# A hybrid streaming-encoder layer on one core: the low parts of the sixteen meta tokens move into the rows of high x

## The chip, the cores and the metric

The kernel runs on one core of one Trainium2 chip. The metric is the device time of one execution in microseconds, the median over several runs. The core has a matrix engine (PE, which loads weights and streams columns of a moving operand past them into PSUM), a vector engine (DVE), a scalar engine (ACT), a general engine (POOL), an engine that only issues transfers (SP), and sixteen DMA engines.

## The reference, cut to what matters

One layer, 512 real tokens behind 16 learned meta tokens, model width 2048. Everything the change touches is the first projection:

```python
meta = jnp.broadcast_to(meta_tokens[None], (bsz, N_META, D_MODEL))
h_res = jnp.concatenate([meta, x], axis=1)          # 16 + 512 rows
hn = _rmsnorm(h_res, norm_in_g[l])
P = hn @ w_in[l]                                    # 2048 -> 65 * 128 columns
Pr, Pc = P[..., :RW_COLS], P[..., RW_COLS:]         # group A: r, k, v, g, two low-rank inputs; group B: B, C, h, gc
...
prev = jnp.pad(Pr[:, :-1], ((0, 0), (1, 0), (0, 0)))
Pr = Pr + (prev - Pr) * mu_shift[l]                 # token shift: token t needs t - 1
...                                                 # RWKV-7 recurrence over r, k, v; gated width-3 convolution over B, C, h, gc
h_res = h_res + mix @ w_out[l]
out = _rmsnorm(h_res, norm_f_g)[:, N_META:]
```

The meta tokens are dropped from the output, so not every projection needs all of them. k, v and the low-rank inputs feed the recurrent state and need all 16. r, g, C and h need only the last two (token shift and convolution look one and two tokens back). B and gc need none.

## The kernel before, in words

**The projection.** Its 65 output tiles of 128 columns are computed one after the other in an order written out as a table (`plan`). Weights are the stationary operand (128 x 128), x is the moving one. Both are fp32 numbers cut into a high and a low part, because a product of two such parts is accurate enough only when three of the four cross products are added: high w by high x, high w by low x, low w by high x. So each of the 16 slices of the contraction (`kt`) takes three matmuls for each column range (`steps`, L319 to L331). The high and low parts of x stand in SBUF for the whole kernel: `xh` and `xl`, 16 rows of 640 numbers per partition each, in each row the 512 real columns first, then the last two meta tokens, then the first fourteen.

**The ranges.** A tile goes to PSUM in one or two banks. k, v and the low-rank tile use `FULL`: columns 0 to 256, and 256 to 528 (256 real and 16 meta). r, g, C and h use `TAIL`: 0 to 256, and 256 to 514. B and gc use `REAL`: 0 to 512 in one bank. There are 17 tiles of the first kind, 32 of the second and 16 of the third. For one tile four slices of the first range are done, then four of the second, four times over; so matmuls of one width stand in chains of twelve.

**Leaving PSUM.** `scaled` (L346) multiplies a tile by the row of token scales `rs` on DVE, real columns and the two groups of meta columns apart, since these go to the front of the result. ACT and DVE then do the token shift, the convolution or the gates.

**The first 50 us.** Four tiles (`lora`, k0, r0, B0) are computed side by side, slice by slice, while x and the first weights arrive. SP issues the transfers in the order of the text: one array `front` in four pieces (the first slice of x with gains and a first weight, three more weights, the second slice with four weights, slices 2 and 3 with eight), then weights and the other slices. ACT and DVE cut x (`split_x`, L205) and weights (`split_piece`, L225) in an order written by hand; ACT also squares x and DVE adds the squares into `accd` for the token scales (`square_x`, L213).

**Order of the rest.** PE runs one hand-made stream: small matmuls of the attention-like parts (`prepare`, `invert`, `recur`) are put into the stream of the projection, and `fill(ns)` issues that many nanoseconds of projection matmuls (counted as 0.43 ns per column) between two steps of them, so that ACT and DVE have time to bring what the next step needs. DVE, ACT and POOL queues outside the hand-ordered stretches are set by a scheduler. From about 841 us on the output projection follows, in the Winograd-like form of seven products; the change does not touch it.

Of the kernel before, what the change touches and what calls it, by code (L numbers as in the profile page):

```python
# [18 lines left out]
P = 128  # L19
# [58 lines left out]
def hymba_kernel(ctx: ExitStack, tc: tile.TileContext, xt, xtok, front, w_in, w_out, pv, lup, cst, msk, gf, out):  # L78
# [75 lines left out]
    xl = xp.tile([P, KT, XROW], F32R, name="xl")  # L154
# [44 lines left out]
    def load_x(tag, a, n):  # L199
        t = view(tag, n * L)  # L200
        nc.sync.dma_start(t.rearrange("p (k l) -> p k l", k=n), xt[:, a : a + n, :])
        for k in range(n):
            raw[a + k] = t[:, k * L : (k + 1) * L]

    def split_x(kt, cols=slice(0, L)):  # L205
        gain = ng[:, kt : kt + 1]
        nc.scalar.activation(xh[:, kt, cols], raw[kt][:, cols], AF.Copy, scale=gain)
        return nc.vector.scalar_tensor_tensor(
            out=xl[:, kt, cols], in0=raw[kt][:, cols], scalar=gain, in1=xh[:, kt, cols].bitcast(F32),
            op0=ALU.mult, op1=ALU.subtract,  # L210
        ).ins

    def square_x(kt, first=False):  # L213
        sq = accd if first else tr(f"sqx{kt}")[:, 0:L]
        nc.scalar.activation(sq, raw[kt], AF.Square)
        if not first:
            nc.vector.tensor_tensor(out=accd, in0=accd, in1=sq, op=ALU.add)
# [15 lines left out]
    F0, F1, F2 = KT + P + L, 4 * P + L, 8 * P + 2 * L  # L233
    fr = [view("bt", F0), view("r0", 3 * P), view("bk", F1), view("gt0", F2)]
# [5 lines left out]
    raw[0], raw[1] = fr[0][:, KT + P : F0], fr[2][:, 4 * P : F1]  # L240
    for k in range(2):
        raw[2 + k] = fr[3][:, 8 * P + k * L : 8 * P + (k + 1) * L]
# [8 lines left out]
    with tc.manual_schedule(engines={mybir.EngineType.DVE, mybir.EngineType.Activation}):  # L251
        split_piece(0, 0, fr[0][:, KT : KT + P])
        split_x(0, slice(0, L // 2))
        split_x(0, slice(L // 2, L))
        for n in (1, 2, 3):
            split_piece(n, 0, fr[1][:, (n - 1) * P : n * P])
        split_x(1)
# [16 lines left out]
        square_x(1)  # L274
        head = split_x(8)
# [38 lines left out]
    FULL = ((0, HALF), (HALF, L))  # L314
    TAIL = ((0, HALF), (HALF, SEQ + 2))
    REAL = ((0, SEQ),)
    PLACED = ((0, SEQ, META), (SEQ, SEQ + 2, META - 2), (SEQ + 2, L, 0))

    def steps(ps, ranges, k4, q, ks=range(4), rs_=range(2)):  # L319
        hi, lo = quarters[q]  # L320
        for r, (a, b) in enumerate(ranges):
            if r not in rs_:
                continue
            for k in ks:
                kt = 4 * k4 + k
                w = slice(k * P, (k + 1) * P)
                for n, (ww, xx) in enumerate(((hi, xh), (hi, xl), (lo, xh))):
                    nc.tensor.matmul(  # L328
                        ps[r], ww[:, w], xx[:, kt, a:b], start=(kt == 0 and n == 0), stop=(kt == KT - 1 and n == 2)
# [16 lines left out]
    def scaled(ranges, ps, dst, base):  # L346
        for (a, b), p in zip(ranges, ps):
            for c, d, t in PLACED:
                c0, d0 = max(a, c), min(b, d)
                if c0 < d0:  # L350
                    o = t + c0 - c - base
                    nc.vector.tensor_tensor(
                        out=dst[:, o : o + d0 - c0], in0=p[:, c0 - a : d0 - a], in1=rs[:, c0:d0], op=ALU.mult
                    )
# [128 lines left out]
    def mains():  # L483
# [5 lines left out]
        for k in range(4):  # L489
            for n, (ps, rg) in enumerate(four):  # L490
                if k == n == 0:
                    hi, lo = quarters[0]
                    for ww, xx, first in ((hi, xh, True), (lo, xh, False), (hi, xl, False)):
                        for p, (a, b) in zip(ps, rg):
                            nc.tensor.matmul(p, ww[:, 0:P], xx[:, 0, a:b], start=first, stop=False)
# [131 lines left out]
    def prepare(i):  # L627
# [7 lines left out]
        fill(FW["start"] if i else 6700)  # L635
# [40 lines left out]
        shift = {0: 2000, 1: 2500, 3: -4000}.get(i, 0)  # L676
# [31 lines left out]
        fill(FW["gram2"] - shift)  # L708
# [757 lines left out]
def _layout(i):  # L1466
# [4 lines left out]
    xt = hres.reshape(L, KT, P).transpose(2, 1, 0)  # L1471
    w = np.asarray(i["w_in"])[0].reshape(KT, P, 65, P).transpose(2, 1, 0, 3).reshape(65, P, DM)
# [28 lines left out]
    front = [pv[:, V_NG : V_NG + KT], first[0][:, 0], xt[:, 0]] + [t[:, 0] for t in first[1:]]  # L1501
# [25 lines left out]
```

## Time and profile before

| | |
|---|---|
| median of 3 runs | 1002.05 us (1001.93 to 1002.06) |
| profiled execution, its own time | 1003.54 us |
| its span, first to last instruction | 1001.7 us, 1.84 us less than its time |
| granted TensorE clock over the span | 0.998 |
| matmuls / weight loads in it | 9723 / 9723 |
| ACT, POOL busy | 393.5 us (39%), 272.3 us (27%) |
| HBM | 137.44 MB read, 36.35 MB written, 173 GB/s over the span |

How to read it: weight loads (PEld) overlap the matmuls, so the two busy times of the matrix engine are not added. The duration that the profile gives one matmul runs from its issue to its modelled end, some 280 ns for 256 columns, while the next one starts after less than half of that; so what a matmul costs is read from the distance between starts, in the timeline, and not from its duration. In the timeline consecutive instructions of one line and the same tiles are merged into one row with a count (x2).

### The profile page before, as it was taken

The page shows a single profiled execution, that of the slowest core. Times are in us where ns is not written, and L with a number is a line of the kernel's source. Part 1 is how long each engine was busy: PE and PEld are TensorE (multiplying, and loading weights), DVE is VectorE, ACT ScalarE, POOL GpSimd, SP SyncE. Part 2 cuts the span into 40 slices and gives each one's busy share as a digit, 9 for nine tenths or more (in the row PEclk, how much of TensorE's full clock was granted, in tenths as well). Part 3 has the DMA queues.
Part 4 walks back from the last instruction along what each step waited for, and adds up shares of the span by engine and source line. Part 5 has one row for each costly group of instructions (what it writes and reads, how often), then busy time and mean ns, then how long its engine had stood idle before and what let it go on. Part 6 is the DMA issues. An engine that isn't in the chain of part 4 may idle for free.

```text
span 1001.7 us, 23771 instructions
## 1 busy us (share of the span) xinstructions
PE 989.9 (99%) x9723; PEld 913.8 (91%) x9723; DVE 687.3 (69%) x1313; ACT 393.5 (39%) x729; POOL 272.3 (27%) x286
## 2 busy tenths in 40 slices
PE   9999999999999999999999999999999999999996
PEld 8999999999998999998999998979888898888886
DVE  7687975588765579744669744335454597999995
ACT  7553423344323434322434322223222325646553
POOL 0123423225332424233423222223332333001001
PEclk9999999999999999999999999999999999999999
DMA  9526576455664373854274846978673698788644
GB/s 335 153 73 167 128 200 162 109 145 126 164 171 149 101 184 105 206 147 119 85 193 102 202 140 175 342 228 255 198 233 86 173 280 228 215 283 228 144 103 168
DMA packets 185181, 175.35 MB, mean 175 GB/s; under 512 B 121584, under 2 KB 142832, under 8 KB 184560
## 3 DMA queue, kind: packets, MB, share of 16 engines
q1 hardware_dynamic: 182480, 164.92, 57.1%
q0 software_dynamic: 2304, 8.39, 4.9%
q8 instruction: 76, 1.25, 0.5%
q10 hardware_dynamic: 288, 0.52, 0.1%
q14 instruction: 33, 0.27, 0.1%
HBM read 137.44 MB, written 36.35 MB: 173 GB/s over the span
## 4 chain that ended last, share of the span: by engine, by line
PE 68%; DVE 1%; DMA 1%; issue 0%; SPq 0%; ACT 0%; DVEq 0%; POOL 0%
PE ps_gc L328 8%; PE M L1243 8%; PE ps_B L328 7%; PE ps_h L328 7%; PE ps_C L328 6%; PE ps_k L328 5%; PE ps_v L328 5%; PE ps_g L328 5%; PE ps_r L328 5%; PE P L1243 4%; PE Q L1243 2%; PE zy L1010 1%; PE zs L1006 1%; PE rz L954 1%; PE g L682 1%; PE end L1450 1%
## 5 line engine op out<-in xcount | busy, mean ns | idle before, releaser
L135 POOL TENSOR_TENSOR w<-wr,w 128x512 fp32r<-128x512 f32 x119 | 174.3, 1466 | 349.7 <-ACT w L134 290.5
L134 ACT CAST w<-wr 128x512 fp32r<-128x512 f32 x252 | 152.8, 618 | 281.9 <-PE ps_k L328 45.4
L135 DVE TENSOR_TENSOR w<-wr,w 128x512 fp32r<-128x512 f32 x133 | 98.7, 747 | 105.5 <-ACT w L134 105.2
L328 PE MATMUL ps_k<-xh,w 128*128 128x256 f32 (+1 forms) x512 | 95.5, 285 | 0.0
L328 PE MATMUL ps_r<-xh,w 128*128 128x256 f32 (+1 forms) x512 | 95.2, 282 | 0.0
L328 PE MATMUL ps_v<-xh,w 128*128 128x272 f32 (+1 forms) x512 | 95.2, 284 | 0.0
L328 PE MATMUL ps_h<-xh,w 128*128 128x258 f32 (+1 forms) x512 | 94.0, 283 | 0.0
L328 PE MATMUL ps_C<-xh,w 128*128 128x258 f32 (+1 forms) x512 | 93.2, 282 | 0.0
L328 PE MATMUL ps_g<-xh,w 128*128 128x258 f32 (+1 forms) x512 | 91.9, 281 | 0.2 <-DVE gt L692 0.2
L328 PE MATMUL ps_B<-xh,w 128*128 128x512 f32 x256 | 83.5, 395 | 0.1
L328 PE MATMUL ps_gc<-xh,w 128*128 128x512 f32 x256 | 81.5, 393 | 0.0
L328 PEld LDWEIGHTS ps_r<-xh,w 128*128 128x128 f32 x512 | 80.4, 190 | 0.3
L328 PEld LDWEIGHTS ps_k<-xh,w 128*128 128x128 f32 x512 | 80.2, 189 | 0.5
L328 PEld LDWEIGHTS ps_h<-xh,w 128*128 128x128 f32 x512 | 79.7, 189 | 0.7
L328 PEld LDWEIGHTS ps_v<-xh,w 128*128 128x128 f32 x512 | 80.1, 189 | 0.3
L328 PEld LDWEIGHTS ps_C<-xh,w 128*128 128x128 f32 x512 | 79.7, 189 | 0.6
L328 PEld LDWEIGHTS ps_g<-xh,w 128*128 128x128 f32 x512 | 79.3, 190 | 0.6 <-issue 0.4
L328 PE MATMUL ps_k<-xl,w 128*128 128x256 f32 (+1 forms) x256 | 72.9, 285 | 0.0
L328 PE MATMUL ps_v<-xl,w 128*128 128x256 f32 (+1 forms) x256 | 72.6, 284 | 0.0
L328 PE MATMUL ps_g<-xl,w 128*128 128x256 f32 (+1 forms) x256 | 72.5, 283 | 0.0
L328 PE MATMUL ps_r<-xl,w 128*128 128x256 f32 (+1 forms) x256 | 72.3, 283 | 0.0
L328 PE MATMUL ps_C<-xl,w 128*128 128x256 f32 (+1 forms) x256 | 72.0, 281 | 0.0
(320 smaller groups left out, 2264.6 us busy)
## 6 DMA issues: line engine op xcount, KB each, us to landing
wr<-in_w_in_dram SPq DMA_DIRECT2D x126, 512.0 KB
ct<-opd SPq DMA_DIRECT2D x64, 288.0 KB
wo<-in_w_out_dram SPq DMA_DIRECT2D x21, 512.0 KB
x<-in_w_out_dram POOLq DMA_DIRECT2D x16, 512.0 KB, 5.7
opd<-ar SPq DMA_DIRECT2D x8, 576.0 KB
opd<-gt SPq DMA_DIRECT2D x16, 288.0 KB
opd<-bt SPq DMA_DIRECT2D x64, 64.0 KB
x<-in_w_out_dram SPq DMA_DIRECT2D x8, 512.0 KB
```

Source lines behind the costliest of these rows:

```text
L134: nc.scalar.copy(hi, rq)
L135: low[q] = eng.tensor_tensor(out=lo, in0=rq, in1=hi.bitcast(F32), op=ALU.subtract).ins
L328: nc.tensor.matmul(ps[r], ww[:, w], xx[:, kt, a:b], start=(kt == 0 and n == 0), stop=(kt == KT - 1 and n == 2))
L682: nc.tensor.matmul(z[h][:, c - c0], bk[hs, c, h : h + 2, :].rearrange("p a s -> p (a s)"), ar[hs, c].rearrange("p a s -> p (a s)"), start= ...
L954: nc.tensor.matmul(z[e][ho if e else hs, 0, k], t[hs, o : o + CH], t[hs, O_V : O_V + CH] if part else st[hs, 4 * e + k], start=(part == 0 ...
L1006: nc.tensor.matmul(d[hs, j], w, x[hs], start=(a == 0), stop=(a == b - 1))
L1010: nc.tensor.matmul(d[ho, j], t[hs, o : o + CH], x[hs], start=(a == 0), stop=(a == b - 1))
L1243: nc.tensor.matmul(bank[s], left(prod, jj, m, s), w, start=(jj == 0 and n == 0), stop=(jj == 7 and n == 2))
L1450: nc.tensor.matmul(ends[part], left("M2", jj, m, 1), w[:, cols], start=(jj == 0 and n == 0), stop=(jj == 7 and n == 2))
```

## The change

The row of `xh` becomes: 512 real columns, the high parts of the last two meta tokens, their low parts, the high parts of the first fourteen, their low parts (544 numbers in the same 640). `xl` keeps only the real columns, 512 to a row. The new function `passes` gives the three matmuls of a slice for a range: high w by `xh` over high and low meta columns (260 or 288 wide), high w by `xl` over the 256 real columns, low w by `xh` up to the last high meta column (258 or 274; the latter also covers the two low columns in between). In the last slice the widest comes last. So the high-by-low product of a meta token lies in PSUM columns of its own, and `scaled` adds the pair with a TENSOR_REDUCE on DVE before it multiplies with `rs`.

At the start, the meta columns of all slices arrive in one piece (`metax`, issued third); `split_meta` multiplies them with the gains and cuts them for slices 1 to 15 in one DVE multiplication and two ACT/DVE pairs. Slice 0 brings its own. Real columns are then cut and squared 512 wide, the squares of the meta columns are summed by a reduce (`square_meta`). Three `fill` amounts of the first head pair move 1 us of projection work from behind the decay scan to ahead of the low-rank product.

```diff
-    xl = xp.tile([P, KT, XROW], F32R, name="xl")
+    xl = xp.tile([P, KT, SEQ], F32R, name="xl")
...
+    HI_A, LO_A, HI_B, LO_B = (slice(*c) for c in ((SEQ, SEQ + 2), (SEQ + 2, SEQ + 4), (SEQ + 4, L + 2), (L + 2, L + META)))
...
+    def split_meta(ks):
+        g = metag[:, ks]
+        nc.vector.tensor_tensor(
+            out=g, in0=metax[:, ks], in1=ng[:, ks].unsqueeze(2).to_broadcast([P, g.shape[1], META]), op=ALU.mult
+        )
+        for t, h, l in ((slice(0, 2), HI_A, LO_A), (slice(2, META), HI_B, LO_B)):
+            nc.scalar.copy(xh[:, ks, h], g[:, :, t])
+            nc.vector.tensor_tensor(out=xh[:, ks, l], in0=g[:, :, t], in1=xh[:, ks, h].bitcast(F32), op=ALU.subtract)
...
+    def square_meta():
+        sq = tr("sqm")[:, 0 : KT * META].rearrange("p (k t) -> p k t", t=META)
+        nc.scalar.activation(sq, metax, AF.Square)
+        nc.vector.tensor_reduce(out=accd[:, SEQ:L], in_=sq.rearrange("p k t -> p t k"), op=ALU.add, axis=AX.X)
...
-    fr = [view("bt", F0), view("r0", 3 * P), view("bk", F1), view("gt0", F2)]
+    fr = [view("bt", F0), view("r0", 3 * P), metax.rearrange("p k t -> p (k t)"), view("bk", F1), view("gt0", F2)]
...
         split_piece(0, 0, fr[0][:, KT : KT + P])
-        split_x(0, slice(0, L // 2))
-        split_x(0, slice(L // 2, L))
+        split_x(0, slice(0, SEQ // 2))
+        x0 = fr[0][:, KT + P : F0]
+        for h, c in ((slice(SEQ // 2, SEQ + 2), slice(SEQ // 2, SEQ + 2)), (HI_B, slice(SEQ + 2, L))):
+            nc.scalar.activation(xh[:, 0, h], x0[:, c], AF.Copy, scale=ng[:, 0:1])
+        real = slice(SEQ // 2, SEQ)
+        for d, c, h in ((xl[:, 0, real], real, real), (xh[:, 0, LO_A], HI_A, HI_A), (xh[:, 0, LO_B], slice(SEQ + 2, L), HI_B)):
+            nc.vector.scalar_tensor_tensor(
+                out=d, in0=x0[:, c], scalar=ng[:, 0:1], in1=xh[:, 0, h].bitcast(F32), op0=ALU.mult, op1=ALU.subtract
+            )
         for n in (1, 2, 3):
             split_piece(n, 0, fr[1][:, (n - 1) * P : n * P])
+        split_meta(slice(1, KT))
         split_x(1)
...
-    FULL = ((0, HALF), (HALF, L))
-    TAIL = ((0, HALF), (HALF, SEQ + 2))
+    FULL = ((0, HALF), (HALF, L + META))
+    TAIL = ((0, HALF), (HALF, SEQ + 4))
     REAL = ((0, SEQ),)
-    PLACED = ((0, SEQ, META), (SEQ, SEQ + 2, META - 2), (SEQ + 2, L, 0))
+
+    def passes(q, r, last=False):
+        (hi, lo), (a, b) = quarters[q], r
+        mid = min(b, SEQ)
+        end = {SEQ + 4: SEQ + 2, L + META: L + 2}.get(b, b)
+        p = [(hi, xh, a, b), (hi, xl, a, mid), (lo, xh, a, end)]
+        return p[1:] + p[:1] if last else p
...
-                for n, (ww, xx) in enumerate(((hi, xh), (hi, xl), (lo, xh))):
+                for n, (ww, xx, a, b) in enumerate(passes(q, part, kt == KT - 1)):
                     nc.tensor.matmul(
-                        ps[r], ww[:, w], xx[:, kt, a:b], start=(kt == 0 and n == 0), stop=(kt == KT - 1 and n == 2)
+                        ps[r][:, 0 : b - a], ww[:, w], xx[:, kt, a:b], start=(kt == 0 and n == 0),
+                        stop=(kt == KT - 1 and n == 2),
                     )
...
         for (a, b), p in zip(ranges, ps):
-            for c, d, t in PLACED:
-                c0, d0 = max(a, c), min(b, d)
-                if c0 < d0:
-                    o = t + c0 - c - base
+            m, o = min(b, SEQ), META + a - base
+            nc.vector.tensor_tensor(out=dst[:, o : o + m - a], in0=p[:, 0 : m - a], in1=rs[:, a:m], op=ALU.mult)
+            for t, n, h, c in ((META - 2, 2, SEQ, SEQ), (0, META - 2, SEQ + 4, SEQ + 2)):
+                if b >= h + 2 * n:
+                    e = tp.tile([P, META], F32, tag="tl", name="tl", bufs=4)[:, 0:n]
+                    nc.vector.tensor_reduce(
+                        out=e, in_=p[:, h - a : h - a + 2 * n].rearrange("p (a t) -> p t a", a=2), op=ALU.add, axis=AX.X
+                    )
                     nc.vector.tensor_tensor(
-                        out=dst[:, o : o + d0 - c0], in0=p[:, c0 - a : d0 - a], in1=rs[:, c0:d0], op=ALU.mult
+                        out=dst[:, t - base : t - base + n], in0=e, in1=rs[:, c : c + n], op=ALU.mult
                     )
...
-        fill(FW["start"] if i else 6700)
+        fill(FW["start"] if i else 7700)
...
-        shift = {0: 2000, 1: 2500, 3: -4000}.get(i, 0)
+        shift = {0: 1000, 1: 2500, 3: -4000}.get(i, 0)
...
-        fill(FW["gram2"] - shift)
+        fill(FW["gram2"] - shift - 1000 * (i == 0))
```

**What moves on PE.** The second range of tile C0, before: `ps_C_1` is its second bank, `w` the slot that holds the high and low part of the weights.

```order
L328 MATMUL ps_C_1_5669<-xh,w_5336 128x258
L328 MATMUL ps_C_1_5669<-xl,w_5336 128x258
L328 MATMUL ps_C_1_5669<-xh,w_5336 128x258 x2
L328 MATMUL ps_C_1_5669<-xl,w_5336 128x258
L328 MATMUL ps_C_1_5669<-xh,w_5336 128x258 x2
```

The same place now; in the k, v and low-rank tiles 288, 256 and 274 stand for 260, 256 and 258.

```order
L361 MATMUL ps_C_1_5767<-xh,w_5430 128x260
L361 MATMUL ps_C_1_5767<-xl,w_5430 128x256
L361 MATMUL ps_C_1_5767<-xh,w_5430 128x258
L361 MATMUL ps_C_1_5767<-xh,w_5430 128x260
L361 MATMUL ps_C_1_5767<-xl,w_5430 128x256
```

The number of matmuls is the same; a chain of twelve equal widths has become a cycle of three widths.

**What moves on DVE at the start**, before: from the first cut of x to the second slice's (`xl<-in_bk`). `in_bt`, `in_r` and `in_bk` are the buffers in which the pieces of `front` arrive.

```order
L208 SCALAR_TENSOR_TENSOR xl<-in_bt,xh 128x264 x2
L228 TENSOR_TENSOR w_144<-in_r_148,w_144 128x128
L228 TENSOR_TENSOR w_145<-in_r_148,w_145 128x128
L228 TENSOR_TENSOR w_146<-in_r_148,w_146 128x128
L208 SCALAR_TENSOR_TENSOR xl<-in_bk,in_bt,xh 128x528
```

The same stretch now:

```order
L210 SCALAR_TENSOR_TENSOR xl<-in_bt,xh 128x256
L278 SCALAR_TENSOR_TENSOR xl<-in_bt,xh 128x256
L278 SCALAR_TENSOR_TENSOR xh<-in_bt,xh 128x2
L278 SCALAR_TENSOR_TENSOR xh<-in_bt,xh 128x14
L244 TENSOR_TENSOR w_144<-in_r_150,w_144 128x128
L244 TENSOR_TENSOR w_145<-in_r_150,w_145 128x128
L244 TENSOR_TENSOR w_146<-in_r_150,w_146 128x128
L217 TENSOR_TENSOR metag<-metax,in_bt 128x240
L222 TENSOR_TENSOR xh<-metag,xh 128x15x2
L222 TENSOR_TENSOR xh<-metag,xh 128x15x14
L210 SCALAR_TENSOR_TENSOR xl<-in_bk,in_bt,xh 128x512
```

Two short cuts of slice 0 and the three instructions of `split_meta` now stand ahead of the second slice; on ACT the two copies of `split_meta` stand between the same neighbours.

35 lines of the change are left out of this document (20 added, 15 removed).

## The prediction

> **What bounds the kernel now.** I read the page first, then the engine waits, then the chain that ended last, then the timeline of PE.
>
> ```profile
> span 1001.7 us, 23771 instructions
> PE 989.9 (99%) x9723; PEld 913.8 (91%) x9723; DVE 687.3 (69%) x1313; ACT 393.5 (39%) x729; POOL 272.3 (27%) x286
> PE pwarm L187 <- DVE cold L184: 1.4, 1, 1.4
> PE zy L1010 <- issue: 1.3, 1, 1.3
> 53.50:618.00 564.50, 564.13 (x5419) 541.48 (x5418) 384.88 (x820) 207.26 (x384) 179.15 (x186) 1.00 0.56 145
> ```
>
> The second PE row is its longest wait after the start, and in the 564.5 us of the middle (columns: PE, PEld, DVE, ACT, POOL) PE shows no gap while DVE is busy 384.88 us. So PE's own stream of matmuls sets the end, and the change is worth what it does to the distance between starts. Four whole tiles from the chain that ended last:
>
> ```profile
> 468.15 11.58 PE ps_k L328 x96
> 530.94 11.53 PE ps_v L328 x96
> 568.47 11.25 PE ps_C L328 x96
> 786.21 10.88 PE ps_gc L328 x48
> ```
>
> gc: 10.88 / 48 = 226.7 ns for 512 columns. C streams 0.4% more columns than gc and takes 3.4% longer. The timeline (first column the start in us) tells which width is dear:
>
> ```profile
> 358.34 0.29 PE L328 MATMUL ps_k<-xl,w 128*128 128x272 f32 x1
> ...
> 359.45 0.29 PE L328 MATMUL ps_k<-xl,w 128*128 128x272 f32 x1
> ...
> 361.16 0.28 PE L328 MATMUL ps_k<-xl,w 128*128 128x256 f32 x1
> ...
> 361.87 0.28 PE L328 MATMUL ps_k<-xl,w 128*128 128x256 f32 x1
> ...
> 419.39 0.28 PE L328 MATMUL ps_C<-xl,w 128*128 128x256 f32 x1
> ...
> 420.41 0.28 PE L328 MATMUL ps_C<-xl,w 128*128 128x256 f32 x1
> ...
> 420.75 0.28 PE L328 MATMUL ps_C<-xl,w 128*128 128x258 f32 x1
> ...
> 421.84 0.29 PE L328 MATMUL ps_C<-xl,w 128*128 128x258 f32 x1
> ```
>
> The matmul with low x is every third one, so from row to row nine starts lie between (six in the second pair). In C: 1.02 / 9 = 113.3 ns for 256 columns, 1.09 / 9 = 121.1 ns for 258. Two columns more cost 7.8 ns. In k: 1.11 / 9 = 123.3 ns for 272, and 0.71 / 6 = 118.3 ns for 256. So 256 columns have a short distance (113) and a long one (118), and both hold for whole chains. 48 x 113.3 + 48 x 121.1 = 11.25 us and 48 x (118.3 + 123.3) = 11.60 us: the tiles are explained. From 272 to 512 a column costs (226.7 - 123.3) / 240 = 0.43 ns; what the change can win is the step just above 256, not columns.
>
> **The change part by part.** The number of matmuls and weight loads stays. TAIL streams 260 + 256 + 258 = 774 columns a slice, as 3 x 258 before; FULL 288 + 256 + 274 = 818 against 816. There are 32 TAIL tiles with 16 slices (512 steps) and 17 FULL ones (272 steps).
>
> *TAIL.* Before 3 x 121.1 = 363.3 ns. Now 258 stays at 121.1, 260 is 121.1 + 2 x 0.43 = 122.0. The open term is a lone 256 between wider ones; the nearest rows are two of the low-rank product (`tz`, 256 wide) between 272s of v:
>
> ```profile
> 62.22 0.28 PE L571 MATMUL tz<-la,luh 128*128 128x256 f32 x1
> 62.34 0.28 PE L572 MATMUL tz<-la,lul 128*128 128x256 f32 x1
> 62.46 0.28 PE L328 MATMUL ps_v<-xl,w 128*128 128x272 f32 x1
> 62.58 0.41 PE L328 MATMUL ps_v<-xh,w 128*128 128x272 f32 x2
> ```
>
> 0.36 us for two 256s and one 272 leaves (360 - 123.3) / 2 = 118.4 each. Bounds 113.3 and 118.4; I take 116, since the neighbours here are nearer to 256 than there. 122.0 + 116 + 121.1 = 359.1: -4.2 ns a step, **-2.15 us** for 512 (bounds -0.9 and -3.5).
>
> *FULL.* Before 369.9 ns. 274 is 123.3 + 0.9 = 124.2. For 288, the line from 272 gives 123.3 + 16 x 0.43 = 130.2; the only 288s of the trace stand on two-column weights:
>
> ```profile
> 359.81 0.30 PE L714 MATMUL n_misc<-sq_h,ones 128*2 128x288 f32 x1
> ...
> 360.34 0.40 PE L717 MATMUL zb<-rk_h,ones 128*128 128x512 f32 x1
> ```
>
> Four in 0.53 us are 132.5 ns. I take 131.3: 131.3 + 116 + 124.2 = 371.5, +1.6 a step, **+0.44 us** for 272 (bounds: 130.2 + 113.3 + 124.2 gives -0.6, 132.5 + 118.4 + 124.2 gives +1.4). The 16 columns of low meta that are moved beside the high ones are streamed all the same; only their place changes.
>
> *The first range.* Its 256-wide chains are not edited, but a chain's distance depends on what ran before it. After twelve 272s it is 118.3 (k above). After a mere pair of 272s (the low-rank product in v at 59.7 us) it is
>
> ```profile
> 59.72 0.29 PE L572 MATMUL tz<-la,lul 128*128 128x272 f32 x1
> ...
> 60.08 0.28 PE L328 MATMUL ps_v<-xl,w 128*128 128x256 f32 x1
> ...
> 60.76 0.28 PE L328 MATMUL ps_v<-xl,w 128*128 128x256 f32 x1
> ```
>
> 0.68 / 6 = 113.3. After the change no chain of twelve wide ones is left; each cycle holds a 256. For FULL (17 x 48 = 816 matmuls) the bounds are no change and -5 ns each, less about a fifth that are short already (v's tile is shorter than k's): -3.2 us. For TAIL (32 x 48 = 1536) it is no change or up to +5 ns each, +7.7 us, if the mixed cycle locks the chain behind it in the long distance. I take **-0.7 us**: the pair of 272s is nearest to the new cycle and speaks for short, but k's whole tile at 118 says that the long distance keeps itself up.
>
> *The first 12 us.* ACT, DVE, PE, then the DMA view of the first 14 us (forty slices of 0.35 us, and the mean):
>
> ```profile
> 9.66 0.74 ACT L207 ACTIVATE xh<-in_gt,in_bt 128x528 fp32r<-128x528 f32 x1 [2.50 <-DMA in_gt<-in_front_dram]
> 6.40 0.77 DVE L208 SCALAR_TENSOR_TENSOR xl<-in_bk,in_bt,xh 128x528 fp32r<-128x528 f32 x1 [0.23 <-ACT xh L207]
> 8.09 0.28 PE L328 MATMUL ps_lora<-xl,w 128*128 128x256 f32 x1
> 10.84 0.28 PE L328 MATMUL ps_lora<-xh,w 128*128 128x256 f32 x1
> 11.25 0.39 PE L328 MATMUL ps_lora<-xl,w 128*128 128x256 f32 x1
> 11.59 0.51 PE L328 MATMUL ps_lora<-xh,w 128*128 128x256 f32 x2
> GB/s 0 0 0 0 8 108 154 361 379 402 418 405 428 416 273 238 261 333 404 357 452 332 284 183 200 223 273 402 331 392 459 459 416 378 394 340 416 398 416 372
> DMA packets 1250, 4.22 MB, mean 302 GB/s; under 512 B 132, under 2 KB 260, under 8 KB 994
> ```
>
> Slice 2 is what PE waits for: 0.41 + 0.34 us between starts instead of 2 x 0.12, so 0.5 us lost, because its transfer lands at 9.66. Now 256 columns of meta (131 KB) go ahead of it, and 48 columns (25 KB) are saved: 106 KB at the 302 GB/s of the first 14 us is 0.35 us. Slice 1 is late too: two short cuts (0.15 us each), then the DVE product of 240 columns (0.42 us), two ACT copies (0.3 and 0.4), a DVE subtraction (0.4) ahead of the cut of slice 1, which then ends near 9.0 in place of 7.17, while PE asks for it at 8.09. That stall of 0.7 to 0.9 us takes the place of the one at slice 2, not of nothing. Together **+0.45 us** (bounds: the transfer alone, at the 400 GB/s that most slices from 3 us on reach, +0.27; both in full, +0.9).
>
> *Leaving PSUM.* 66 reduces more (two for each FULL tile, one for each TAIL tile) on DVE, in the class of
>
> ```profile
> L789 DVE TENSOR_REDUCE y<-prod 72x4 f32<-72x8 f32 x32 | 5.0, 156 | 0.9
> L352 DVE TENSOR_TENSOR pr_k<-ps_k,rs 128x14 f32<-128x14 f32 x8 | 1.3, 161 | 0.0
> ```
>
> 66 x 0.16 = 10.5 us of DVE, hidden under PE: DVE is idle a third of the middle, and two pairs of banks let PE run a tile (11 us) ahead. Queued behind a tile's multiplication are the shift and the products of the next head pair, later by 0.3 us. The place with least cover is the first pair, where the low-rank product waits for lora's shift; the 1 us of `fill` that is moved ahead of it is cover for that. **+0.1 us**; without cover 0.3 us for each of eight pairs, +2.4. Squares and cuts of x are 16 columns narrower and the reduce of `square_meta` takes that back: 0. The shorter rows of `xl` (512 in place of 640) cost nothing in any row: 0.
>
> Sum: -2.15 + 0.44 - 0.7 + 0.45 + 0.1 = -1.86 us on the span of 1001.7, so 999.8. The profiled execution has 1.84 us around its span; the median of the runs, 1002.05, lies 1.5 us under that execution, and I carry the difference over to it: **1000.2 us**.
>
> **The rivals.** *The short distance everywhere* (996 to 998): lone 256s at 113.3 and FULL's first chains short, -3.5 - 0.6 - 3.2 + 0.3 = -7.0 in full, about -5 for most of it: 997. For it: the pair in v, after which the chain is short. Against: the `tz` rows at 118.
>
> *The long distance everywhere* (slower): a 256 behind the mixed cycle stays at 118.3 through its chain of twelve, in TAIL tiles too, where it is 113.3 now. With a share s of TAIL's chains locked the time moves by -1.2 + 7.7 s: it decides from s = 0.15 on, is measurable from 0.41, and gives 1004.7 at one half, 1008.6 at all. For it: k, where it never leaves that state. Against: chains behind 258s, the closest width, are short in every C tile.
>
> *Columns alone count* (the change does not do what it says): what 258 pays over 256 is a price of the change of width or of the phase, so a cycle of three widths pays it again on each. Then 2 x 0.43 x 272 = +0.2, with +0.45 and +0.1: 1002.8. For it: the `tz` rows, where 256 gained only 5 of 10 ns. The Trainium skill has this as a rule (TensorE: Matmul & The Clock Gate, "Wait — 56ns, not 53.3ns?"): the distance is the columns at 2.4 GHz plus about 2.5 ns, whatever the width. By it 256, 258 and 512 would take 109.2, 110.0 and 215.8 ns; the trace has 113.3, 121.1 and 226.7, so it agrees for none of them, and the measured step decides against it here.
>
> **How the numbers follow.** Forecast 0.36, short everywhere 0.24, long everywhere 0.26, columns alone 0.14. About 0.2%, 2 us, is what a measurement can tell from no change. The forecast's own range is 998.8 to 1001.6, with 0.14 of its 0.36 below 1000.05; short everywhere is all faster; long everywhere is 0.21 slower and 0.05 within; columns alone 0.12 within and 0.02 slower. Faster 0.38, within 0.39, slower 0.23. The range 996 to 1005 leaves out the extreme third of each outer rival.
>
> **What would show it.** In the chain, a tile of C at 48 x 113.3 + 16 x 359.1 = 11.18 us against 11.25, k at 48 x 117.5 + 16 x 371.5 = 11.58. In the timeline: the row of `xl` at 256 with 116 ns to the next start, and whether the chains of twelve run at 113 or 118. At the start: PE's stall at slice 1 and not at slice 2, slice 3 some 0.45 us later. The forecast is wrong if C tiles take 11.4 us or more, or if PE shows waits for DVE's `tl` or `pr` tiles.

## The result, and the profile after

| | before | after |
|---|---|---|
| median of five runs each, us | 1002.05 (1001.49 to 1003.10) | 1006.28 (1005.76 to 1006.67) |
| profiled execution, its own time, us | 1003.54 | 1006.28 |

The ratio of the times is 1.0041, its 95% interval 1.0027 to 1.0056: slower by 0.4%. The forecast was 1000.2 with a range of 996 to 1005. The profiled execution of before was 1.5 us above the median of its kernel; the after one is its median. So 4.2 us are to be found, of which the two spans show 2.8.

The page of after, its span and its busy times, and its row of the 564.5 us of the middle (windows; PE, PEld, DVE, ACT, POOL):

```profile
span 1004.5 us, 23845 instructions
PE 990.9 (99%) x9723; PEld 913.6 (91%) x9723; DVE 696.3 (69%) x1385; ACT 393.9 (39%) x733; POOL 273.4 (27%) x286
57.70:622.20 564.50, 561.66 (x5394) 538.47 (x5393) 389.22 (x867) 205.96 (x381) 179.24 (x186) 1.00 0.56 145
```

The window that was without a gap before (0.37 us idle) now has 2.84 us of idle PE, and DVE is 4.3 us busier in it. The page's sums say no more; the engine waits do (total, times, longest):

```profile
...
PE g L720 <- DVE pr_v L390: 1.3, 1, 1.3
PE zy L1048 <- issue: 0.9, 1, 0.9
PE ps_g L361 <- DVE gt L730: 0.5, 1, 0.5
PE g L720 <- DVE pr_k L390: 0.4, 1, 0.4
PE ps_lora L361 <- ACT w L243: 0.3, 1, 0.3
...
PE ps_lora L361 <- DVE xl L210: 0.2, 1, 0.2
PE g L720 <- DVE bk L698: 0.2, 1, 0.2
```

Five of these seven rows were not in before's answer. `g` at L720 are the grams: 36 small matmuls that multiply the key-like and the query-like arrays of a head pair (`bk` and `ar`); DVE takes the products on into `gt`. Why they wait for `pr_v` and `pr_k`, the emptied projection tiles, shows in the timeline at pair 3 (start in us, duration in us), after:

```profile
251.93 2.24 PE L720 MATMUL g<-ar,bk 64*128 64x128 f32 x34 [0.21 <-DVE bk L698]
...
253.03 0.42 DVE L383 TENSOR_TENSOR pr_v<-ps_v,rs 128x256 f32<-128x256 f32 x1
253.36 1.44 DVE L640 TENSOR_TENSOR rk_l<-r,rk_h 128x512 fp32r<-128x512 f32 x1
254.72 0.41 DVE L383 TENSOR_TENSOR pr_v<-ps_v,rs 128x256 f32<-128x256 f32 x1
255.06 0.24 DVE L387 TENSOR_REDUCE tl<-ps_v 128x2 f32<-128x4 f32 x2
...
255.44 0.46 PE L720 MATMUL g<-ar,bk 64*128 64x128 f32 x2 [1.27 <-DVE pr_v L390]
```

and before:

```profile
249.37 2.85 PE L682 MATMUL g<-ar,bk 64*128 64x128 f32 x36
250.72 0.89 DVE L352 TENSOR_TENSOR pr_v<-ps_v,rs 128x256 f32<-128x256 f32 x4
```

The ninth chunk of a gram (`ze`, the last two of the 36) lies in two of the four banks that the projection tiles use in turn, the two that tile v has just filled. DVE must have emptied them. Its queue puts the 1.44 us of `rk_l` between the two halves of v; the second half and the two sums then hold the bank until 255.30, and PE stands still until 255.44. Before, v was emptied in one piece by 251.6, while the grams ran.

At pair 0 the same thing happens to k: the cut of a low-rank weight, `lul`, stands between its two halves, and the last two grams wait. Before, `lul` came ahead of both halves, and k was empty by 82.1, while grams that started at 80.95 ran. The 36 take 3.1 us now, 2.3 before; the other 0.3 us of pair 0 are lost behind them, partly to a wait for ACT.

```profile
82.07 2.27 PE L720 MATMUL g<-ar,bk 64*128 64x128 f32 x34
82.61 0.41 DVE L383 TENSOR_TENSOR pr_k<-ps_k,rs 128x256 f32<-128x256 f32 x1
82.95 1.16 DVE L633 TENSOR_TENSOR lul<-lur,luh 128x256 fp32r<-128x256 f32 x1
84.02 0.41 DVE L383 TENSOR_TENSOR pr_k<-ps_k,rs 128x256 f32<-128x256 f32 x1
...
84.74 0.46 PE L720 MATMUL g<-ar,bk 64*128 64x128 f32 x2 [0.40 <-DVE pr_k L390]
```

Where the 4.2 us arise, from the start of a tile's first matmul in PE's timeline (after minus before):

| at | before, us | after minus before, us | what lies ahead of it |
|---|---|---|---|
| B0, fourth quarter | 37.20 | +1.10 | the first 14 us |
| r1 | 77.64 | +1.08 | |
| v1 | 92.37 | +2.28 | grams of pair 0: +1.2 |
| g2 | 242.79 | +2.26 | |
| g3 | 257.48 | +3.89 | grams of pair 3: +1.6 |
| gc | 605.21 | +4.14 | 348 us of tiles: +0.25, of which 0.2 is a tile B that waits for the low part of its weights |
| gc, next | 661.00 | +3.07 | small matmuls of the recurrence, which waited 1.1 us longer in before's execution |

Head, pair 0, pair 3 and the stretch of tiles make 1.1 + 1.2 + 1.6 + 0.25 = 4.15 us in these two executions; the 1.1 of the head is at the top of its scatter (below), so the medians' 4.2 can't be split as finely. In the 348 us the tiles themselves should have won: three of them in the chain of after,

```profile
273.89 11.41 PE ps_C L361 x96
472.35 11.54 PE ps_k L361 x96
572.42 11.27 PE ps_C L361 x96
```

against the forecast's 11.18 for C and 11.58 for k. k comes out near its forecast, C has won nothing, and some C take 11.4.

### The profile page after: what moved, and what is told of

It reads as the page before. It is cut to its first block, busy times and chain, and to the rows that moved or that the text cites. A ratio compares the mean times of both kernels' runs of the same rounds, so it can differ in the third digit from the quotient of the medians.

```text
span 1004.5 us, 23845 instructions
## 1 busy us (share of the span) xinstructions
PE 990.9 (99%) x9723; PEld 913.6 (91%) x9723; DVE 696.3 (69%) x1385; ACT 393.9 (39%) x733; POOL 273.4 (27%) x286
## 4 chain that ended last, share of the span: by engine, by line
PE 88%; DVE 5%; DMA 2%; POOL 1%; issue 1%; SPq 1%; ACT 1%; DVEq 0%; POOLq 0%; ACTq 0%
PE ps_h L361 9%; PE ps_gc L361 9%; PE ps_B L361 9%; PE ps_C L361 8%; PE ps_g L361 8%; PE M L1281 8%; PE ps_r L361 8%; PE ps_v L361 7%; PE ps_k L361 7%; PE P L1281 4%; PE Q L1281 2%; PE g L720 1%; PE ps_lora L361 1%; PE zy L1048 1%; PE zs L1044 1%
## 5 line engine op out<-in xcount | busy, mean ns | idle before, releaser
L361 PE MATMUL ps_k<-xh,w 128*128 128x256 f32 (+2 forms) x512 | 95.7, 285 | 0.0
L361 PE MATMUL ps_v<-xh,w 128*128 128x256 f32 (+2 forms) x512 | 95.1, 286 | 0.0
L361 PE MATMUL ps_h<-xh,w 128*128 128x256 f32 (+2 forms) x512 | 94.6, 283 | 0.0
L361 PE MATMUL ps_r<-xh,w 128*128 128x256 f32 (+2 forms) x512 | 94.1, 281 | 0.0
L361 PE MATMUL ps_C<-xh,w 128*128 128x256 f32 (+2 forms) x512 | 93.4, 282 | 0.0
L361 PE MATMUL ps_g<-xh,w 128*128 128x256 f32 (+2 forms) x512 | 92.2, 281 | 0.5 <-DVE gt L730 0.5
L361 PE MATMUL ps_g<-xl,w 128*128 128x256 f32 x256 | 71.2, 281 | 0.0
L361 PE MATMUL ps_h<-xl,w 128*128 128x256 f32 x256 | 71.1, 281 | 0.0
L361 PE MATMUL ps_r<-xl,w 128*128 128x256 f32 x256 | 71.0, 280 | 0.0
L361 PE MATMUL ps_C<-xl,w 128*128 128x256 f32 x256 | 71.0, 280 | 0.0
```

The source lines that it names most:

```text
L361: nc.tensor.matmul(ps[r][:, 0 : b - a], ww[:, w], xx[:, kt, a:b], start=(kt == 0 and n == 0), stop=(kt == KT - 1 and n == 2),)
```

## The experiments

All ratios are against the kernel before on the same chip, with 95% intervals; "leaves out" names the product that a kernel doesn't compute.

**1. The sums alone taken away.** The change, with the high meta columns alone scaled.

```diff
-                    nc.vector.tensor_reduce(
-                        out=e, in_=p[:, h - a : h - a + 2 * n].rearrange("p (a t) -> p t a", a=2), op=ALU.add, axis=AX.X
-                    )
...
-                        out=dst[:, t - base : t - base + n], in0=e, in1=rs[:, c : c + n], op=ALU.mult
+                        out=dst[:, t - base : t - base + n], in0=p[:, h - a : h - a + n], in1=rs[:, c : c + n], op=ALU.mult
```

> The changed kernel without the sums of high and low meta columns: the TENSOR_REDUCEs are left out, the high columns alone are scaled, so the product of high w with low meta is missing from the output. DVE has as many instructions per tile as before. Theory sums (the reduces make the emptying of a PSUM bank longer, and the last grams of pairs 0 and 3 wait for that bank): the two waits of 1.2 and 1.6 us go, PE's offset against the kernel before is about 1.1 us at the first tile of v and stays there, 1003.4 us. Theory order (the scheduler has put DVE's queue in another order ahead of the grams; in pair 3 this kernel has that same new order): the wait at pair 3 stays at 1.3 us or more, 1005 us or above.

1002.99 us, ratio 1.0001 (0.9992 to 1.0010): the theory of the sums held. Nothing is lost at pair 0, 0.3 us at pair 3:

```profile
PE g L716 <- DVE pr_v L386: 0.4, 1, 0.4
```

Without the sums 3.3 us of the median are back (4.0 by the two ratios). In the traces 2.5 us are back at the two grams and 0.7 in the first 14 us, which differ from run to run (below). DVE's queue at pair 3 still has `rk_l` between the halves of v (at 250.22, 1.43 us); at pair 0 k is emptied in one piece again.

**2. Low x cut at 512.** The kernel before with its low-x matmul 256 wide, and nothing else.

```diff
+                    e = min(b, SEQ) if n == 1 else b
...
-                        ps[r], ww[:, w], xx[:, kt, a:b], start=(kt == 0 and n == 0), stop=(kt == KT - 1 and n == 2)
+                        ps[r][:, 0 : e - a], ww[:, w], xx[:, kt, a:e], start=(kt == 0 and n == 0), stop=(kt == KT - 1 and n == 2)
```

> The kernel before with one thing alone: the matmul with low x stops at column 512 (the product of high w with low meta is left out). Widths per step are 258, 256, 258 and 272, 256, 272; DVE's queue, the first 12 us and everything else stand as before. Theory give-back (the lone 256 is cheaper, and the chains of twelve 256s behind it become dearer in r, g, C, h and cheaper in k, v): r, g, C, h tiles stay at 11.25 to 11.4 us, k and v tiles fall from 11.55 to about 11.3, in all 997 to 1000. Rival (a step's widths cost what they cost, 113 for 256 wherever it stands): C tiles 11.12, k tiles 11.4, 995 to 997. Rival (nothing can be won by the width of low x): within 1 us of 1002.

998.46 us, ratio 0.9961 (0.9946 to 0.9976). This is the gain that the forecast had in mind, and more. So a lone 256 between two 258s does save time; what the change adds to it takes the gain away. The time lies in the range of the give-back theory by luck: the chains behind the lone 256 became no dearer (345.3 before, 343.5 here, in the table under 5, 6, 10), r, g, C, h tiles fell to 11.20 us on the mean, and k, v tiles only to 11.47.

**3. Sums alone.** The kernel before with 66 sums whose results nobody reads.

```diff
+                    if c >= SEQ:
+                        n = d0 - c0
+                        e = tp.tile([P, META], F32, tag="tl", name="tl", bufs=4)[:, 0:n]
+                        nc.vector.tensor_reduce(
+                            out=e, in_=p[:, b - a - 2 * n : b - a].rearrange("p (a t) -> p t a", a=2), op=ALU.add, axis=AX.X
+                        )
```

> The kernel before with one thing alone: each group of meta columns gets a TENSOR_REDUCE of a pair of columns of its bank into a scratch tile ahead of its multiplication, 66 in all, with the changed kernel's instruction and sizes (their sums are not used). Stream and start stand as before. Theory sums or order: waits of 1 to 1.6 us appear at the grams of pair 0 or pair 3, 1004 to 1005 us. Rival (the waits come from the stream's or the start's delay, not from the emptying): no new wait, 1002.0 to 1002.5.

1003.90 us, ratio 1.0007 (0.9997 to 1.0016): 0.66 us at pair 3, nothing at pair 0. The result lies between the two theories: a wait does appear, half as long as the first one said.

```profile
PE g L688 <- DVE pr_v L358: 0.8, 1, 0.8
```

The scheduler has put `lul` and `rk_l` between the halves of k and v here as in the change. At pair 0 that costs nothing, since the fill amounts are the old ones and DVE is through with k (82.2) before the grams get to the shared banks.

**4. The meta split of one slice first.** The change, with `split_meta` for slice 1 alone ahead of its cut.

```diff
-        split_meta(slice(1, KT))
+        split_meta(slice(1, 2))
...
+        split_meta(slice(2, KT))
```

> The changed kernel with split_meta for slice 1 alone ahead of the cut of slice 1, and for slices 2 to 15 behind the weights of slice 1. Theory queue (DVE and ACT cut fifteen slices' meta columns while PE waits for slice 1): PE's offset at 37 us falls from 1.1 to 0.5 or 0.6, in all 1005.7. Rival (the transfer of the meta columns ahead of slice 1 sets it): the offset stays at 1.0 to 1.1.

1005.78 us, ratio 1.0033 (1.0020 to 1.0047). The first 37 us cost 1.11 us here, 1.10 in the change; both waits at the grams are as in the change. But the 1.11 is made up differently: PE runs at half pace until 7.5 us (6.2 at the latest in the change; last section), then waits no longer at slice 1 and is at slice 2 0.27 us earlier than the change, and loses that again at slice 2. The profiled execution is also 1.2 us slower than the median, and the median is what the first theory said (1005.7). So this run does not decide whether that queue piece matters.

**5, 6, 10. Which of the wider matmuls eats the gain.** Run 5 is run 2 with high w by high x two columns wider in r, g, C and h. Run 6 is run 1 with these tiles back at 258/256/258, so that 288 is left in k, v and the low-rank tile. Run 10 is run 5 with the 256 last in each step. The three edits, in this order:

```diff
+                three = ((hi, xh, b + 2 * (b == SEQ + 2)), (hi, xl, min(b, SEQ)), (lo, xh, b))
+                for n, (ww, xx, e) in enumerate(three[1:] + three[:1] if kt == KT - 1 else three):
...
-    TAIL = ((0, HALF), (HALF, SEQ + 4))
+    TAIL = ((0, HALF), (HALF, SEQ + 2))
...
+                order = (0, 2, 1) if kt == 0 else (2, 1, 0) if kt == KT - 1 else (2, 0, 1)
```

> The kernel before with low x cut at column 512 (as in the run that gave 998.46 us), and in r, g, C and h the matmul of high w and high x two columns wider: 260/256/258 a step as in the change, with no sums, no new meta columns at the start, and k, v and the low-rank tile as in that run. The high-w by low-meta product is left out; the two more columns of PSUM are not read. Measured mean distances of all r, g, C and h tiles (three chained 256s plus one step): 706.3 ns before, 706.3 in the change, 700.1 in that run. Theory 'the wider step makes the chains behind it long': the sum comes back to about 706 ns, chains at 115.5 to 116 instead of 114.5, so +3.2 us: about 1001.6 us. Rival 'two columns cost two columns': +0.86 ns for each of 512 steps, 0.44 us: about 998.9 us, and the lost gain of the change is then not in this step.

> The change without its sums (the run that gave 1002.99 us), and r, g, C and h back at 258/256/258 a step; k, v and the low-rank tile keep 288/256/274. The high-w by low-meta product is left out. Theory 'the wider step makes the chains behind it long': r, g, C and h tiles fall to the 700 ns of the run with the narrow low x, -3.2 us: about 999.8 us, and k, v and the low-rank tile stay at 721 ns (717 in that run; 272 steps, so 288 columns cost 1.2 us in all). Rival 'two columns cost two columns': about 1002.5 us.

> The kernel before with 260/256/258 in r, g, C and h (the run that gave 1001.77 us; high w by low meta left out), with the order inside each step of a slice turned: low w, high w by high x, high w by low x, so that the 256 stands last in each cycle and the chain of twelve follows a 256; first and last slice keep the widest at the end that PSUM needs. Theory 'a chain takes over the pace of what stands just ahead of it': chains behind a 256 are short (113.5) and the loss of the two columns goes: about 998.5 to 999.5 us. Rival 'the pace is set by the mix of three widths, not by the last one': chains stay at 115.5 to 116 on the mean, whole tiles at 118: about 1001.8 us.

Measured: run 5 1001.77 us, ratio 0.9993 (0.9984 to 1.0002); run 6 1000.75, 0.9977 (0.9968 to 0.9986); run 10 1003.02, 0.9998 (0.9987 to 1.0008). The mean distance between starts over all tiles after 53 us, as nanoseconds per slice (three of the first range and the three of the step), and how many of 124 chains of twelve 256s run at 116.5 ns or more:

| | r, g, C, h: chain + step | long chains | k, v: chain + step |
|---|---|---|---|
| before | 345.3 + 361.0 = 706.3 | 24 | 350.9 + 370.7 = 721.6 |
| the change | 347.7 + 358.6 = 706.3 | 47 | 346.7 + 374.5 = 721.2 |
| run 2: 258/256/258 | 343.5 + 356.6 = 700.1 | 21 (of 123) | 350.0 + 366.7 = 716.7 |
| run 5: 260/256/258 | 348.0 + 358.6 = 706.6 | 48 | 350.8 + 366.3 = 717.1 |
| run 6: 258/256/258, k and v 288 | 343.9 + 356.7 = 700.6 | 22 | 346.8 + 374.5 = 721.3 |
| run 10: 258/260/256 | 347.8 + 359.5 = 707.3 | 53 | 350.5 + 367.0 = 717.5 |

Two columns more in one of six matmuls cost 6 ns a slice, 3 us in the whole: 2 ns in the step and 3.8 to 4.5 in the chains behind it. Runs 5 and 6 agree from both sides: the wider step makes the chains behind it long. In the change and in run 5, 8 of the 31 r, g, C, h tiles run long in all four chains; before, in run 2 and in run 6 none does. Run 10's theory falls: the pace of a chain is not taken from the matmul just ahead of it. What it is taken from stays open; that it comes with the cycle 260/256/258 is shown. PE's timeline of the change at tile C (low x, every third matmul):

```profile
273.85 0.28 PE L361 MATMUL ps_C<-xl,w 128*128 128x256 f32 x1
...
275.26 0.28 PE L361 MATMUL ps_C<-xl,w 128*128 128x256 f32 x1
275.62 0.28 PE L361 MATMUL ps_C<-xl,w 128*128 128x256 f32 x1
...
276.70 0.28 PE L361 MATMUL ps_C<-xl,w 128*128 128x256 f32 x1
```

and of run 2 at the same tile:

```profile
269.27 0.28 PE L329 MATMUL ps_C<-xl,w 128*128 128x256 f32 x1
...
270.63 0.28 PE L329 MATMUL ps_C<-xl,w 128*128 128x256 f32 x1
270.99 0.28 PE L329 MATMUL ps_C<-xl,w 128*128 128x256 f32 x1
...
272.06 0.28 PE L329 MATMUL ps_C<-xl,w 128*128 128x256 f32 x1
```

In each piece the first pair of rows spans twelve matmuls of the chain, the second nine of the step. Chain: 1.41 / 12 = 117.5 ns in the change, 1.36 / 12 = 113.3 in run 2. Step: 1.08 / 9 = 120.0 and 1.07 / 9 = 118.9.

**7. More projection work ahead of the grams.** The change, with 2 us more of `fill` ahead of the grams of pairs 0 and 3 and 2 us less behind.

```diff
-        shift = {0: 1000, 1: 2500, 3: -4000}.get(i, 0)
+        shift = {0: 3000, 1: 2500, 3: -2000}.get(i, 0)
```

> The change with 2 us more of projection matmuls ahead of the grams of pairs 0 and 3, and 2 us less behind them; nothing else differs. Theory 'the grams wait for a PSUM bank that DVE empties later because of the sums': the waits of 1.2 and 1.6 us go, 1006.28 - 2.8 = about 1003.5 us, and no wait for pr_k or pr_v shows at the grams. Rival 'a wait that only moves': DVE is late for the whole pair, and PE waits for the products that follow (the decay and bonus products, the second gram) as long as it did before the gram: 1005.5 to 1006.3 us, with a new wait behind the gram of about the same length.

1008.10 us, ratio 1.0054 (1.0040 to 1.0068): the rival held, and at pair 3 it is worse than that.

```profile
PE ps_g L361 <- DVE gt L730: 3.5, 1, 3.5
PE n_misc L752 <- DVE gt L730: 0.7, 1, 0.7
```

The grams no longer wait; the next projection tile does, 3.5 us, for the banks that hold the ninth chunk until DVE has multiplied it into `gt`. The four banks are a ring in which tile, gram and tile follow each other, and DVE sets its pace here. Filling PE's time ahead of one turn only brings it to the next turn too early.

**8. The old fill amounts of the first pair.**

```diff
-        fill(FW["start"] if i else 7700)
+        fill(FW["start"] if i else 6700)
-        shift = {0: 1000, 1: 2500, 3: -4000}.get(i, 0)
+        shift = {0: 2000, 1: 2500, 3: -4000}.get(i, 0)
-        fill(FW["gram2"] - shift - 1000 * (i == 0))
+        fill(FW["gram2"] - shift)
```

> The change with the fill amounts of the first head pair as they were before it (6700 ahead of its low-rank product, 2000 more ahead of its grams, and as much as before behind them); sums, rows of x and the start as in the change. Theory 'the moved microsecond makes the first pair late': its low-rank product comes 1 us earlier and so does the whole DVE chain behind it, the 1.2 us that PE loses between the tiles r1 and v1 go: about 1005.1 us, with the 1.6 us of pair 3 still there. Rival 'the sums alone': 1006.3 us, the same 1.2 us between r1 and v1, or a new wait of the low-rank product for lora's shift.

1004.81 us, ratio 1.0022 (1.0012 to 1.0031). The number came as the first theory said, the trace as the rival did: the 1.2 us between r1 and v1 go, and 1.0 us appears ahead of k1, where the low-rank product waits for lora's shift. The rest of the difference is pair 3, 0.7 us in place of 1.6, in a queue that the scheduler had ordered anew. `rk_l` still stands between the halves of v there (251.80, 1.43 us), but DVE comes to them earlier relative to PE: a product ahead of them takes 1.05 us, and 2.14 in the change (last section).

```profile
PE tz L609 <- DVE la L431: 0.8, 1, 0.8
PE g L720 <- DVE pr_v L390: 0.7, 1, 0.7
```

So the moved microsecond covers one wait of the first pair and opens another: it makes the low-rank product, and DVE's chain behind it, 1 us later, while the grams keep their place.

**9. The sums on POOL.** ACT copies the meta columns out of PSUM, POOL adds and scales them.

```diff
-                    nc.vector.tensor_reduce(
-                        out=e, in_=p[:, h - a : h - a + 2 * n].rearrange("p (a t) -> p t a", a=2), op=ALU.add, axis=AX.X
-                    )
-                    nc.vector.tensor_tensor(
+                    z = tp.tile([P, 2 * META], F32, tag="tz", name="tz", bufs=4)[:, 0 : 2 * n]
+                    nc.scalar.copy(z, p[:, h - a : h - a + 2 * n])
+                    nc.gpsimd.tensor_tensor(out=e, in0=z[:, 0:n], in1=z[:, n : 2 * n], op=ALU.add)
+                    nc.gpsimd.tensor_tensor(
```

> The change with the sums off DVE: ACT copies the high and low meta columns out of PSUM, POOL adds the pair and multiplies with the token scales (99 short DVE instructions fewer than the change has, 66 reduces and 66 short products of DVE and 33 more than the kernel before had products for are gone from DVE). Everything is computed. Theory 'DVE is the engine that is late at the grams': the waits of 1.2 and 1.6 us fall as in the run without sums (none and 0.3 us): 1003.0 to 1003.5 us. Rival 'the new order of the queues is late, whoever adds': POOL's and ACT's queues are as full there, the shift of k and v waits for POOL in place of DVE, and the waits stay: 1005.5 to 1006.5 us or more.

1016.02 us, ratio 1.0131 (1.0117 to 1.0145). The rival held, ten microseconds worse than the change. At pair 0, 5.9 us:

```profile
86.44 0.25 ACT L388 COPY tz<-ps_k 128x4 f32<-128x4 f32 x2 [2.94 <-DVE pr_k L383]
86.68 0.36 POOL L389 TENSOR_TENSOR tl<-tz 128x2 f32<-128x2 f32 x2 [1.49 <-ACT tz L388]
87.00 0.37 POOL L390 TENSOR_TENSOR pr_k<-tl,rs 128x2 f32<-128x2 f32 x2
87.40 0.74 ACT L399 ACTIVATE sh_k<-pr_k,pvt 128x528 f32<-128x528 f32 x1 [0.71 <-POOL pr_k L390]
```

DVE stands still for 1.8 us of it, waiting for ACT's shift of k. Fewer DVE instructions, but two more handovers in a chain in which every link waits for the last.

**11, 12, 13. The place in DVE's queue.** The emptying of PSUM (`scaled`) is built at a higher priority for the scheduler: in the change (11), in the change with the old fill amounts of run 8 (12), and in the kernel before (13).

```diff
+        with ahead():
             for (a, b), p in zip(ranges, ps):
```

> The change with everything that empties a projection tile out of PSUM (products and sums) given a higher priority in the scheduler of DVE's queue; nothing else differs. In the queue of pair 3 the emptying of v's tile now stands ahead of the product of r and the cuts of its squares and of rk; in pair 0 the queue is as in the change. Theory 'the gram waits because the bank's release stands late in DVE's queue': the 1.3 us wait for pr_v goes, pair 3 costs 0.2 to 0.5 us instead of 1.6, and pair 0 its 1.2 us as before: about 1005.0 us. Rival 'DVE as a whole is late there': the release comes earlier but what the gram or the next tile needs (bk, gt) later; pair 3 costs 1.2 us or more: 1006 us or more.

> The run before, with the fill amounts of the first pair as they were before the change as well (the run with these alone gave 1004.81 us). Theory of the queue: the 0.7 us that pair 3 cost in that run go too, the 1.0 us that the low-rank product of pair 0 waits for lora's shift stays: about 1004.2 us. Rival (DVE as a whole is late): 1004.8 us or more. Neither theory expects it below the 1002.5 us of the kernel before.

> The kernel before with the emptying of PSUM at the higher priority in the scheduler of DVE's queue, and nothing else. Theory 'the stream of the change nets zero; what the last run won it won from the order of DVE's queue': the 0.9 us at pair 3 are won here as well, 1000.7 to 1001.9 us, a ratio of 0.9985 to 0.9995 as in the last run. Rival 'the reshaped stream wins once nothing waits': this kernel stays at 1.000 (1002.0 to 1003.0 us), since PE waits for nothing at pair 3 in the kernel before.

Measured: run 11 1004.77 us, ratio 1.0011 (1.0002 to 1.0021); run 12 1001.77, 0.9987 (0.9978 to 0.9996); run 13 1001.59, 0.9980 (0.9971 to 0.9989). Run 11 came as the theory of the queue said: pair 3 costs 0.1 us (its grams don't wait, the next tile does, 1.0 us for `gt`), pair 0, where `lul` still stands between the halves of k, 1.2. In run 12 no gram waits and no low-rank product; PE's longest waits are the start and one "issue":

```profile
PE pwarm L187 <- DVE cold L184: 1.4, 1, 1.4
PE zy L1049 <- issue: 1.1, 1, 1.1
PE ps_B L361 <- DVE w L135: 0.2, 1, 0.2
PE ps_lora L534 <- DVE xh L278: 0.2, 1, 0.2
```

It does all of the change's sums, and neither theory had it below the kernel before. DVE in run 12 at pair 3:

```profile
246.49 0.43 DVE L384 TENSOR_TENSOR pr_v<-ps_v,rs 128x256 f32<-128x256 f32 x1
248.34 0.41 DVE L384 TENSOR_TENSOR pr_v<-ps_v,rs 128x256 f32<-128x256 f32 x1
248.68 0.24 DVE L388 TENSOR_REDUCE tl<-ps_v 128x2 f32<-128x4 f32 x2
...
251.29 0.68 DVE L641 TENSOR_TENSOR rk_l<-r,rk_h 128x512 fp32r<-128x512 f32 x1
```

The second half of v is last read at 248.9, ahead of `rk_l` and 0.5 us before the grams start; in the change it was 255.3, 3.4 us after they started. Run 13 says where run 12's gain is from: the kernel before wins as much by the same line. Its grams at pair 3 now run in 2.28 us, where they took 2.85 with no wait in the engine's answer, and g3 starts 0.9 us earlier:

```profile
249.51 2.28 PE L683 MATMUL g<-ar,bk 64*128 64x128 f32 x36
```

From g3 to gc (605 us) run 13 keeps its distance to before (-0.79 to -0.81) and run 12 loses 0.26 of its own (-0.78 to -0.52), as the change did. Most of that is tile B's wait for `w`, 0.24 us in run 12 and 0.07 in run 13. The reshaped stream itself wins nothing.

## Why the prediction was wrong

**What bounds the kernel** was right: PE's stream, and the step just above 256 columns. Run 2 shows the step's worth, 4 us. The forecast was a gain of 1.9 us, and 4.2 were lost. Of these 6 us about 2.7 are the grams, 2.3 the stream and 0.65 the head of this execution.

**Leaving PSUM, "hidden under PE", +0.1 us: this step failed.** Its cover was "two pairs of banks let PE run a tile (11 us) ahead". At the grams there is no such lead, since the ninth chunk takes two of these four banks. The measured price is 2.8 us (1.2 and 1.6), near the +2.4 that the prediction named for the case without cover but put aside; that is chance, since it had 0.3 us at each of eight pairs and the loss is at two. It looked at DVE's load (a third idle) where DVE's order and lateness at the grams decided: the sums cost 2.5 us at the grams of the change (run 1), 0.7 in the old stream (run 3), nothing at the higher priority and the old fill amounts (run 12).

At pair 0 it takes two things together: `lul` between the halves of k (run 3 has that with the old fill amounts and loses nothing) and the moved microsecond, which the prediction counted as cover (run 1 has that, without `lul` there and without the sums, and loses nothing). At pair 3, `rk_l` between the halves costs 0.3 us without sums (runs 1 and 6), and 0.7 with them (runs 3 and 8). The other 0.9 of the 1.6 goes with a DVE that is later there; the product of 2.14 us stands in its queue in the change and in runs 4 and 7, and takes 1.05 in runs 1, 3 and 8. That the product is what makes DVE late is read from these rows; no run changes it alone.

The line that would have shown it is before's own gram row, 2.85 us at pair 3, with v's emptying in the middle of it.

**TAIL, -2.15 us: mis-sized, and given back.** The step took 358.6 ns (359.1 forecast), but by luck: the lone 256 cost 118.6 (116 forecast, 118.4 its upper bound), and the 258 119.3 (121.1). But 363.3 for before was read from the middle of one chain, and the mean over all tiles is 361.0, mostly since a 258 just behind a 256 is cheaper (115.4 ns, 120.8 behind another 258). So the step won 2.4 ns, 1.2 us. The chains behind it went from 345.3 to 347.7 per slice: 2.4 x 512 = 1.2 us lost. This is the rival of the long distance everywhere, at a share of (47 - 24) / 124 = 0.19 more long chains; the forecast had zero for TAIL. Runs 5 and 6 show that the two low columns do it.

**FULL, +0.44 us: mis-sized.** Its step rose from 370.7 to 374.5, 3.8 ns and 1.0 us. The 288s cost 134.4 ns on the mean (131.3 forecast, 132.5 its upper bound). **FULL's first range, -0.7 us, was right in kind:** 350.9 to 346.7, -1.1 us. That k's tile comes out at 11.54 (11.58 forecast) is these two errors against each other. Together the stream gives -1.2 + 1.2 + 1.0 - 1.1 = -0.1 us, where -2.4 was forecast.

**The first 12 us, +0.45 us: right in kind, 1.1 in this execution.** PE waits at slice 1, for a weight's high part and for low x, and no longer at slice 2 (in runs 4, 6, 8 and 11 it comes to slice 1 so late, 8.9 to 9.3 us, that it doesn't wait there either):

```profile
9.10 0.38 PE L361 MATMUL ps_lora<-xh,w 128*128 128x256 f32 x1 [0.34 <-ACT w L243]
9.70 0.39 PE L361 MATMUL ps_lora<-xl,w 128*128 128x256 f32 x1 [0.21 <-DVE xl L210]
```

Over the profiled kernels the start costs 0.2 to 1.1 us with the new head (nine kernels) and 0.05 to 0.5 with the old one (five); the means, 0.6 and 0.3, differ by 0.3 us. The rest is scatter between executions: run 8 has the change's own instructions there and costs 0.6.

**The chances.** The rivals held one that was half right on the chains, and none on the grams; "PE shows waits for DVE's tl or pr tiles" stood only in the list of what would make the forecast wrong.

## What to carry to other kernels

Before work is put on an engine as "hidden", ask what it holds while it waits in the queue: where a later, unlike user shares the PSUM bank, PE pays for a late emptying, 1.6 us at pair 3. Ask it of the place in the queue and of the time at which the engine gets there, not of the engine's load, and when sums are added, look at how the scheduler reorders the rest; raising the priority of what releases a bank was worth as much here as the whole change was meant to be. And measure a width in its neighbourhood: two thirds of what two columns cost lay in the matmuls behind them.

## What the runs showed that I had not expected

- Chains of 256 have two paces, 113.3 and 118 ns, and in the change can keep one for a whole tile; two columns more in the matmuls between them doubled the number of long ones (24 to 47 of 124).
- PE can start at half pace: in run 2 matmuls of 256 columns are 210 ns apart at 6.4 us, before 110 ns at 5.9, with a granted clock of 1.00 in both windows. How long it lasts differs between executions of the same instructions, until 6.2 us at the latest in the change and 7.6 in run 8, and is part of the scatter of the first 12 us.

```profile
6.38 0.42 PE L329 MATMUL ps_k<-xh,w 128*128 128x256 f32 x1
6.59 0.32 PE L329 MATMUL ps_k<-xl,w 128*128 128x256 f32 x1
```

- POOL can hold DVE up. In the change the product at 244.45 takes 2.14 us, and 1.05 before (at 242.90): POOL's `w` runs from 243.20 to 245.68, and 245.68 + 1.05 = 246.7 is nearly the product's end, 246.6.

```profile
244.45 2.14 DVE L812 TENSOR_TENSOR prod<-d,y 72x512 f32<-72x512 f32 x1
243.20 2.48 POOL L135 TENSOR_TENSOR w<-wr,w 128x512 fp32r<-128x512 f32 x1
```

The Trainium skill (SBUF — State Buffer, "Terms") says that the two engines share a port pair which one of them holds for a whole instruction while the other is fully blocked; these rows agree with it. It is one more way in which DVE's order, and not its load, set when v's tile left PSUM.
